# A decoder trunk whose feed-forward first parts go from six feature tiles to five, with the lambda vectors in another buffer

## The chip, the cores and the metric

The kernel runs on one core of a Trainium2 chip. The core has five engines that work side by side: TensorE (PE in the profile; its weight loads are shown apart as PEld), VectorE (DVE), ScalarE (ACT), GpSimd (POOL) and SyncE (SP), which here only issues transfers. The metric is the device time of the whole program in microseconds, as the median of its runs. One execution was also recorded by the hardware profiler; every row of the profile comes from that one.

## The reference

Two layers, each with two gated feed-forward blocks (FFNs) of half weight around a token mixer. The sequence is 512 long, the model width 1024, the FFN width 2816.

```python
def swiglu(h, w_gate, w_up, w_down):
    return (jax.nn.silu(h @ w_gate) * (h @ w_up)) @ w_down

for l in range(DEPTH):                                   # DEPTH = 2
    x = x + 0.5 * swiglu(rms_norm(x, ffn1_norm[l]), ffn1_w_gate[l], ffn1_w_up[l], ffn1_w_down[l])
    h = rms_norm(x, mix_norm[l])
    a, g, q, k, v = jnp.split(h @ w_in[l], splits, axis=-1)
    conv_out = conv_module(a, g, conv_w[l], conv_b[l], conv_norm[l])
    ...
    lam = (jnp.exp(jnp.sum(lambda_q1[l] * lambda_k1[l]))
           - jnp.exp(jnp.sum(lambda_q2[l] * lambda_k2[l])) + lam_init)
    diff_out = diff_attention(q, k, v, rel_bias, lam, lam_init, subln_norm[l])
    x = x + jnp.concatenate([conv_out, diff_out], axis=-1) @ w_out[l]
    x = x + 0.5 * swiglu(rms_norm(x, ffn2_norm[l]), ffn2_w_gate[l], ffn2_w_up[l], ffn2_w_down[l])
```

So there are four FFNs, and the lambda vectors are needed only in the mixers.

## The kernel before

**Layout and precision.** The activations stay on the chip with the features on the partitions: x is 8 tiles of 128 x 512 (`x[:, k, :]`). Every large product is done three times in a reduced format, as high x high, high x low and low x high: ScalarE makes the high part as a copy, VectorE the low part as a difference (`parts_of`, L95 to L97), for the weights as they arrive and for the activations (`acth`, `actl`; `hh`, `hl`). Weights come through rings of five raw buffers (`wraw`) and four split ones (`whi`, `wlo`), and a pair of smaller ones (`wraw2`, `whi2`, `wlo2`).

**An FFN** (`ffn`, L399) handles its 22 feature tiles of 128 in three parts, listed in `PARTS`. For each part it first makes the gated hidden tiles (gate and up products, silu, product), keeps them as `hh0, hl0, hh1, ...`, and then multiplies them with the down weights: for each of the 8 output tiles m it sums the part's feature tiles in one PSUM bank (`ps_d`) and adds the result to x (L465). `gather` (L105) collects the down weights eight blocks at a time, in the order of their use, so a block of weights can end within an output tile.

**Plain and seven-product tiles.** The feature tiles of the first part (`m < PLAIN`) are plain: gate and up are two products over 8 tiles of the input with 512 columns each (`products`). They use x times the gain without the row scale; the scale `r` is multiplied in when they leave PSUM (L443, L445). The tiles of the later parts use `seven` (L352): the input is cut into halves in features and in positions, and a 2 x 2 block product of gate and up is done with seven products of 4 tiles and 256 columns. For it `sums` (L120) loads and adds weights, with one accumulating DMA and two adds on GpSimd (L137, L142, L143), and `Halves` (L311) makes the sums of the input: eight scaled tiles `hn` (L328), and from them `th` and `tl` (L332 to L337). `settle` (L339) later overwrites `acth` and `actl` with the split of `hn`, once the plain tiles have read the old ones. This VectorE and ScalarE work runs beside the plain tiles and the first down.

**The scale of the rows.** `rows_rstd` (L206) turns the sums of squares round on TensorE (`ps_rows`), adds them on VectorE (`rowv`, L214 and L215) and takes the power on GpSimd (`rs_y`, L203). `spread` (L218) puts the result on a diagonal (`diag`, L230; a high and a low one when split) and multiplies by ones (`ps_spread`, L234), so that ScalarE can copy the scale of each position to all partitions (`rb`, L238). In the first FFN it stands in the middle of the third tile's second product, before its fourth step; its place in TensorE's order is pinned.

**Once, in the first FFN.** When it reaches feature tile 4, `ffn` calls `make_scalars` (L492) and `make_bias` (L472). `make_scalars` loads, for each layer, the four lambda vectors by a GpSimd DMA (`lamv`, L498), multiplies them on GpSimd (L500), sums them on VectorE (L502) and takes the exponential on ScalarE (L504). The buffer of `lamv` is that of `ssum`, the sums of squares, and there is one of it.

**Order.** The program is written in plain order. A planner with its own estimate of durations then sets the order of the instructions on each engine, apart from a few matmuls that are pinned, and adds the waits. Each engine and each DMA queue takes its instructions in that order. PSUM has two banks each for three tags (`sc`, `po`, `mm`) that tiles and down products use in turn.

Of the kernel before, what the change touches and what calls it, by code (L numbers as in the profile page):

```python
# [11 lines left out]
F32 = mybir.dt.float32  # L12
# [6 lines left out]
P = 128  # L19
DEPTH = 2  # L20
SEQ = 512
# [19 lines left out]
HS = SEQ // 2  # L41


PARTS = ((0, 6), (6, 8), (14, 8))
PLAIN = PARTS[0][1]

SPACE = 392
# [14 lines left out]
def lambda_init(layer):  # L62
    return 0.8 - 0.6 * math.exp(-0.3 * layer)
# [3 lines left out]
def trunk(ctx: ExitStack, tc: tile.TileContext, xt, par, lamv, relb, onehot,  # L67
# [7 lines left out]
    wp = ctx.enter_context(tc.tile_pool(name="wp", bufs=1))  # L75
    tmp = ctx.enter_context(tc.tile_pool(name="tmp", bufs=2))
# [3 lines left out]
    def f32(ap):  # L80
        return ap.bitcast(F32)
# [96 lines left out]
    for half in range(2):  # L178
        h, kk = slice(half * 512, (half + 1) * 512), range(half * KT // 2, (half + 1) * KT // 2)
# [16 lines left out]
    def col(l, name, i=0):  # L196
        c = _AT[name] + i
        return pars[l][:, c : c + 1]
# [42 lines left out]
    class Prep:  # L241


        def __init__(self, l, gain):
            self.l, self.gain = l, gain
            self.hi, self.lo = acth, actl
            self.s = tmp.tile([P, SEQ], F32, tag="ssum", name="ssum", bufs=1)
# [63 lines left out]
    class Halves:  # L311
# [4 lines left out]
        def __init__(self, fp, pr, r):  # L316
            self.th = fp.tile([P, 3, KT // 2, HS], F32R, tag="th", name="th")
            self.tl = fp.tile([P, 3, KT // 2, HS], F32R, tag="tl", name="tl")

            self.whole = []  # L320
            free = [(fp, tag, 1) for tag in ("hh6", "hh7", "hl6", "hl7")]
            free += [(wp, tag, 2) for tag in ("whi2", "wlo2") for _ in range(2)]
            a, b = slice(0, HS), slice(HS, SEQ)
            for j in range(KT // 2):
                for k in (j, j + KT // 2):
                    pool, tag, bufs = free.pop()
                    h = pool.tile([P, SEQ], F32, tag=tag, name="hn", bufs=bufs)
                    V.scalar_tensor_tensor(h, x[:, k, :], col(pr.l, pr.gain, k), r, op0=ALU.mult, op1=ALU.mult)  # L328
                    self.whole.append((k, h))
                (_, ha), (_, hb) = self.whole[-2:]  # L330
                t = fp.tile([P, 3, HS], F32, tag="ht", name="ht", bufs=2)
                V.tensor_tensor(t[:, 1], hb[:, b], ha[:, b], op=ALU.subtract)  # L332
                V.tensor_tensor(ha[:, b], ha[:, a], ha[:, b], op=ALU.subtract)
                V.scalar_tensor_tensor(t[:, 0], ha[:, b], -1.0, hb[:, b], op0=ALU.mult, op1=ALU.subtract)
                V.scalar_tensor_tensor(t[:, 2], t[:, 0], -1.0, hb[:, a], op0=ALU.mult, op1=ALU.subtract)
                S.activation(self.th[:, :, j, :], t, AF.Copy)
                V.tensor_tensor(self.tl[:, :, j, :], t, f32(self.th[:, :, j, :]), op=ALU.subtract)  # L337
# [61 lines left out]
    def ffn(pr, gu, dn, after, lead=None, aside=None):  # L399
        with tc.tile_pool(name="ffn", bufs=1) as fp:  # L400
            r = halves = None
            for m0, many in PARTS:
                hh, held, late = [], [], []
# [88 lines left out]
    def make_scalars():  # L492
        for l in range(DEPTH):

            t = tmp.tile([P, SEQ], F32, tag="ssum", name="lamv", bufs=1)
            lv = t[:, : 4 * HD].rearrange("p (n d) -> p n d", n=4)
            pr = t[:, 4 * HD : 6 * HD].rearrange("p (n d) -> p n d", n=2)
            nc.gpsimd.dma_start(lv, lamv[l].partition_broadcast(P))  # L498
            for n in range(2):
                G.tensor_tensor(pr[:, n, :], lv[:, 2 * n, :], lv[:, 2 * n + 1, :], op=ALU.mult)  # L500
            d = small.tile([P, 2], F32, tag="lamd", name="lamd", bufs=1)
            V.tensor_reduce(d, pr, axis=AX.X, op=ALU.add)  # L502
            e = small.tile([P, 2], F32, tag="lame", name="lame", bufs=1)
            S.activation(e, d, AF.Exp)  # L504
            nl = const.tile([P, 1], F32, tag=f"nlam{l}", name=f"nlam{l}")
            V.scalar_tensor_tensor(nl, e[:, 1:2], -lambda_init(l), e[:, 0:1], op0=ALU.add, op1=ALU.subtract)
            nlam.append(nl)
            g = const.tile([P, 2], F32, tag=f"gq{l}", name=f"gq{l}")
            G.memset(g, 0.0)
            for m in range(2):  # L510
                d = slice(m * HD, (m + 1) * HD)
                G.tensor_tensor(g[d, m : m + 1], col(l, "q_norm")[d], col(l, "k_norm")[d], op=ALU.mult)
            G.tensor_scalar(g, g, -math.sqrt(HD), None, op0=ALU.mult)
            gq.append(g)
            g = const.tile([P, 1], F32, tag=f"gsub{l}", name=f"gsub{l}")
            G.tensor_scalar(g, col(l, "subln_norm"), math.sqrt(VD) * (1.0 - lambda_init(l)), None, op0=ALU.mult)
            gsub.append(g)
            g = const.tile([P, CT], F32, tag=f"ghalf{l}", name=f"ghalf{l}")
            c = _AT["conv_norm"]
            G.tensor_scalar(g, pars[l][:, c : c + CT], 0.5, None, op0=ALU.mult)  # L520
            ghalf.append(g)
            c = _AT["conv_w"]
            G.tensor_scalar(pars[l][:, c : c + CT * TAPS], pars[l][:, c : c + CT * TAPS], 0.5, None, op0=ALU.mult)
# [298 lines left out]
    def aside():  # L822
        make_scalars()
        make_bias()
# [92 lines left out]
```

## Time and profile before

| what | value |
|---|---|
| median of three runs | 1805.56 us (1805.36 to 1805.93) |
| the profiled execution | 1803.93 us, of which the span is 1802.1 us |
| TensorE | busy 99% of the span, 10,692 matmuls, granted clock 1.00 |
| VectorE, ScalarE, GpSimd | 67%, 49%, 36% |
| DMA | 228 MB, 127 GB/s on average |

The busy time of an engine is a sum over the span; a matmul's listed duration is its latency, and matmuls follow each other faster than that. In the chain of work that ended last, a piece stands with its start, its length and its instructions. In the list of waits, a row names the engine, the tile and line that waited, then what released it, and total time, count and longest wait. In the rows in order of time, the bracket at the end gives the engine's idle time before the row and what ended it.

### The profile page before, as it was taken

The numbers are of one execution on the slowest core, as the hardware profiler recorded it, in microseconds if no ns is written. First come the engines' busy times: TensorE is split into PE (matmuls) and PEld (weight loads), VectorE is DVE, ScalarE is ACT, GpSimd is POOL, SyncE is SP. The second block draws the span as 40 slices with busy tenths as digits, with TensorE's granted clock in tenths as the row PEclk, the third lists the DMA queues.
The fourth block names the chain that finished last, engine by engine and source line by source line (L and its number), as shares of the span: only waits on it lengthen the run. The fifth ranks groups of instructions, "written<-read, shape, count | busy, mean of one in ns | idle before, by whom it ended". The sixth has DMA issues, their size and how long they took to land.

```text
span 1802.1 us, 27871 instructions
## 1 busy us (share of the span) xinstructions
PE 1785.1 (99%) x10692; PEld 1584.0 (88%) x10692; DVE 1200.5 (67%) x1838; ACT 883.3 (49%) x1450; POOL 640.3 (36%) x448
## 2 busy tenths in 40 slices
PE   8999999999999999999999999999999999999999
PEld 6899899888778889899888998998887888998997
DVE  6957466568867857557576684665788587575662
ACT  5546345445854436346434462554558354463551
POOL 4125123269942024133100341332797330241320
PEclk9999999999999999999999999999999999999999
DMA  6456456333212446546333574654231133564561
GB/s 229 127 129 184 134 152 175 117 105 94 71 46 84 111 112 175 164 124 188 121 94 106 128 200 107 171 169 129 71 108 56 48 105 96 146 179 132 152 174 49
DMA packets 106022, 228.06 MB, mean 127 GB/s; under 512 B 11575, under 2 KB 29254, under 8 KB 105888
## 3 DMA queue, kind: packets, MB, share of 16 engines
q1 hardware_dynamic: 86880, 190.88, 32.7%
q0 software_dynamic: 18720, 35.23, 12.0%
q8 instruction: 84, 1.38, 0.3%
q14 instruction: 50, 0.41, 0.1%
q10 hardware_dynamic: 288, 0.16, 0.0%
HBM read 224.12 MB, written 3.42 MB: 126 GB/s over the span
## 4 chain that ended last, share of the span: by engine, by line
PE 95%; DVE 2%; issue 1%; ACT 1%; DMA 0%; POOL 0%; ACTq 0%; DVEq 0%; POOLq 0%
PE ps_pair L369 36%; PE ps_d L163 9%; PE ps_d L159 9%; PE ps_d L162 9%; PE ps_pair L163 6%; PE ps_pair L162 6%; PE ps_pair L159 6%; PE ps_pair L582 2%; PE ps_pair L583 2%; PE ps_pair L581 2%; PE ps_out L159 1%; PE ps_out L162 1%; PE ps_sc L699 1%; PE ps_out L163 1%; DVE actl L252 1%; PE ps_v L611 1%
## 5 line engine op out<-in xcount | busy, mean ns | idle before, releaser
L96 ACT ACTIVATE whi<-wraw 128x512 fp32r<-128x512 f32 (+1 forms) x580 | 458.7, 814 | 643.7 <-PE ps_d L162 225.7
L97 DVE TENSOR_TENSOR wlo<-wraw,whi 128x512 fp32r<-128x512 f32 (+1 forms) x536 | 510.4, 974 | 191.3 <-ACT whi L96 186.2
L369 PE MATMUL ps_pair<-acth,wlo 128*128 128x256 f32 x1024 | 289.8, 283 | 0.0
L369 PE MATMUL ps_pair<-actl,whi 128*128 128x256 f32 x1024 | 289.8, 283 | 0.0
L369 PE MATMUL ps_pair<-acth,whi 128*128 128x256 f32 x1024 | 289.7, 283 | 0.0
L162 PE MATMUL ps_d<-hl,whi 128*128 128x512 f32 x704 | 274.0, 389 | 0.0
L163 PE MATMUL ps_d<-hh,wlo 128*128 128x512 f32 x704 | 272.7, 389 | 0.0
L159 PE MATMUL ps_d<-hh,whi 128*128 128x512 f32 x704 | 268.7, 389 | 0.0
L137 POOL DMA_DIRECT2D wraw<-in_gu x64 | 76.3, 1193 | 457.8 <-DMA wraw<-in_gu 209.9
L369 PE MATMUL ps_pair<-th,wlo 128*128 128x256 f32 x768 | 217.3, 283 | 0.0
L369 PE MATMUL ps_pair<-tl,whi 128*128 128x256 f32 x768 | 217.2, 283 | 0.0
L369 PE MATMUL ps_pair<-th,whi 128*128 128x256 f32 x768 | 217.2, 283 | 0.0
L142 POOL TENSOR_TENSOR wraw<-wraw 128x512 f32<-128x512 f32 x64 | 95.5, 1492 | 314.9 <-DMA wraw<-in_gu 277.2
L159 PE MATMUL ps_pair<-acth,whi 128*128 128x512 f32 x512 | 200.0, 394 | 5.8 <-ACT whi L96 5.7
L162 PE MATMUL ps_pair<-actl,whi 128*128 128x512 f32 x512 | 200.4, 392 | 0.3 <-DVE actl L252 0.2
L163 PE MATMUL ps_pair<-acth,wlo 128*128 128x512 f32 x512 | 199.6, 391 | 0.7 <-DVE wlo L97 0.7
L369 PEld LDWEIGHTS ps_pair<-actl,whi 128*128 128x128 f32 x1024 | 196.6, 192 | 0.3
L369 PEld LDWEIGHTS ps_pair<-acth,whi 128*128 128x128 f32 x1024 | 196.6, 192 | 0.3
L369 PEld LDWEIGHTS ps_pair<-acth,wlo 128*128 128x128 f32 x1024 | 196.6, 192 | 0.0
L465 DVE SCALAR_TENSOR_TENSOR x<-ps_d,x 128x512 f32<-128x512 f32 x96 | 65.0, 688 | 196.0 <-PE ps_d L163 196.0
L163 PEld LDWEIGHTS ps_d<-hh,wlo 128*128 128x128 f32 x704 | 132.2, 188 | 27.0
L159 PEld LDWEIGHTS ps_d<-hh,whi 128*128 128x128 f32 x704 | 132.2, 188 | 26.9
(172 smaller groups left out, 3316.6 us busy)
## 6 DMA issues: line engine op xcount, KB each, us to landing
wraw<-in_gu SPq DMA_DIRECT2D x108, 512.0 KB, 3.6
wraw<-in_gu SPq DMA_DIRECT2D x200, 256.0 KB, 4.1
wraw<-in_gu POOLq DMA_DIRECT2D x64, 512.0 KB, 5.8
wraw<-in_wqkv SPq DMA_DIRECT2D x24, 512.0 KB, 3.6
wraw<-in_dn SPq DMA_DIRECT2D x52, 192.0 KB, 3.3
wraw<-in_wag SPq DMA_DIRECT2D x16, 512.0 KB, 3.7
wraw<-in_wout SPq DMA_DIRECT2D x16, 512.0 KB, 3.6
wraw<-in_dn SPq DMA_DIRECT2D x24, 320.0 KB, 3.5
```

The costliest lines, as they stand in the source:

```text
L96: S.activation(hi, raw, AF.Copy)
L97: (eng or V).tensor_tensor(out=lo, in0=raw, in1=f32(hi), op=ALU.subtract)
L137: nc.gpsimd.dma_start(two.rearrange("p (b c) -> p b c", b=2), u[:, h[0]].unsqueeze(1).broadcast_to([P, 2, 512]), accum_op=ALU.add)
L142: G.tensor_tensor(more[:, h[0]], two[:, h[1]], whole[:, h[0]], op=ALU.add)
L159: first = T.matmul(ps, wh, xh, start=start, stop=False)
L162: T.matmul(ps, wh, xl, start=False, stop=False)
L163: T.matmul(ps, wl, xh, start=False, stop=stop)
L369: mm = T.matmul(ps, l, r, start=first and i == j == 0, stop=False, skip_group_check=True)
L465: V.scalar_tensor_tensor(x[:, m, :], ps, 0.5, x[:, m, :], op0=ALU.mult, op1=ALU.add)
L581: T.matmul(ps[n], xh[:, t], wh, start=k == 0, stop=False)
L582: T.matmul(ps[n], xh[:, t], wl, start=False, stop=False)
L583: T.matmul(ps[n], xl[:, t], wh, start=False, stop=k == KT - 1)
```

## The change

`PARTS` becomes 5, 8 and 9 feature tiles. So feature tile 5 is no longer plain but a seven-product tile, in the second part, and the third part starts a tile earlier and has nine. With nine tiles there are buffers `hh8` and `hl8`. The eight `hn` tiles of `Halves` take `hh5` to `hh8` and `hl5` to `hl8`, which the first part does not use; before, four of them had lain in the two buffers each of `whi2` and `wlo2`. The lambda vectors take the buffer of the (high) diagonal, of which there is also one.

```diff
-PARTS = ((0, 6), (6, 8), (14, 8))
+PARTS = ((0, 5), (5, 8), (13, 9))
 PLAIN = PARTS[0][1]
...
             self.whole = []
-            free = [(fp, tag, 1) for tag in ("hh6", "hh7", "hl6", "hl7")]
-            free += [(wp, tag, 2) for tag in ("whi2", "wlo2") for _ in range(2)]
+            free = [f"{t}{n}" for t in ("hh", "hl") for n in range(5, 9)]
             a, b = slice(0, HS), slice(HS, SEQ)
             for j in range(KT // 2):
                 for k in (j, j + KT // 2):
-                    pool, tag, bufs = free.pop()
-                    h = pool.tile([P, SEQ], F32, tag=tag, name="hn", bufs=bufs)
+                    h = fp.tile([P, SEQ], F32, tag=free.pop(), name="hn")
                     V.scalar_tensor_tensor(h, x[:, k, :], col(pr.l, pr.gain, k), r, op0=ALU.mult, op1=ALU.mult)
...
     def make_scalars():
         for l in range(DEPTH):
 
-            t = tmp.tile([P, SEQ], F32, tag="ssum", name="lamv", bufs=1)
+            t = tmp.tile([P, SEQ], F32, tag="diag", name="lamv", bufs=1)
             lv = t[:, : 4 * HD].rearrange("p (n d) -> p n d", n=4)
```

## The prediction

> **What bounds the kernel now.** I read the page's busy shares first, then the chain that ended last, then TensorE's waits, and then the stretches that the change touches.
>
> ```profile
> PE 1785.1 (99%) x10692; PEld 1584.0 (88%) x10692; DVE 1200.5 (67%) x1838; ACT 883.3 (49%) x1450; POOL 640.3 (36%) x448
> PE 95%; DVE 2%; issue 1%; ACT 1%; DMA 0%; POOL 0%; ACTq 0%; DVEq 0%; POOLq 0%
> PE ps_pair L159 <- ACT whi L96: 5.7, 1, 5.7
> PE ps_out L159 <- ACT acth L683: 2.5, 2, 1.3
> PE ps_spread L234 <- DVE diag L230: 1.8, 1, 1.8
> ```
>
> TensorE is busy 99% of the span and carries 95% of the chain. Its longest waits are the start (5.7 us) and, for this change, 1.8 us for the first scale's diagonal. So the end moves with the number of matmuls times their spacing, and with any new wait on TensorE. The stretches around the parts, and one of plain matmuls:
>
> ```profile
> 50.00:91.00 41.00, 41.00 (x182) 33.50 (x181) 36.25 (x62) 22.71 (x33) 5.69 (x6) 1.00 0.47 136
> 112.00:200.00 88.00, 88.00 (x706) 86.70 (x705) 59.10 (x87) 50.28 (x86) 28.81 (x18) 1.00 0.63 170
> 236.00:325.00 89.00, 89.00 (x710) 87.52 (x709) 59.12 (x85) 49.59 (x85) 28.14 (x18) 1.00 0.61 164
> 50.03 0.39 PE L163 MATMUL ps_pair<-acth,wlo 128*128 128x512 f32 x1
> 56.83 0.39 PE L163 MATMUL ps_pair<-acth,wlo 128*128 128x512 f32 x1
> 112.16 76.31 PE ps_pair L369 x636
> 1673.95 76.31 PE ps_pair L369 x636
> ```
>
> The columns of the first three are the stretch, its length, then busy time with the instruction count for TensorE, its weight loads, VectorE, ScalarE and GpSimd, then granted clock, DMA share and GB/s. TensorE is full in the end of the plain part (50 to 91) and in both parts of eight seven-product tiles (from 112 and 236), at clock 1.00, with DMA at 0.61 to 0.63. VectorE is the nearest other engine only in the plain part: 36.25 of 41 us.
>
> **The swap of one tile in each of four FFNs.** Feature tile 5 changes from plain to seven products. Plain is 2 x 8 x 3 = 48 matmuls of 512 columns. From 50.03 to 56.83 lie 30 of them: 6.80 / 30 = 0.2267 us each, 10.88 us per tile (their 0.39 us is latency, which overlaps). Seven products are 7 x 4 x 3 = 84 matmuls of 256 columns: 76.31 / 636 = 0.120 us, 10.08 us per tile. The gain is 0.80 us, and 4 x 0.80 = 3.2 us. The down products stay 22 x 8 x 3 per FFN (5 + 8 + 9 against 6 + 8 + 8), so their PE time does not move.
>
> The Trainium skill, "TensorE: Matmul & The Clock Gate", section "Back-to-back issue gap", speaks against the swap by one of its rules: a sustained stream is spaced by weight load and matmul together, with 81 ns for 128 columns and 131 ns for 512; an estimate on a straight line between them gives 98 ns for 256, 8.2 us for 84 against 6.3 us for 48, a loss of 1.9 us per tile. The section's other rule, the isolated gap of 518 and 262 cycles, makes 10.4 against 9.2 us, at 2.4 GHz, an estimate of 4.8 us gained in all. The trace agrees with the sign of the second and is 5 to 10% above its gaps.
>
> **What the extra seven-product tiles bring beside TensorE.** Per FFN: one more accumulating DMA and two adds on GpSimd, six splits on ScalarE and on VectorE in place of two, and 0.75 MB more of weights than the plain tile's 1 MB. They run at the end of a part whose eight tiles show TensorE full at the DMA share and VectorE share above, so nothing lands on the path: zero. If that cover failed, the price would be the wait of one tile's operands; none shows in the eight such parts (the chain has eight runs of 636 matmuls in 76.31 us, the first and the last above), and I keep 1 us per FFN as an upper end. The down weights need 20 more SP issues, since runs of five and nine blocks are cut differently; each is short and hidden by the five-deep ring:
>
> ```profile
> wraw<-in_dn SPq DMA_DIRECT2D x36, 64.0 KB, 2.7
> ...
> 42.42 0.69 DVE L443 TENSOR_TENSOR gs<-ps_pair,rb 128x512 f32<-128x512 f32 x1
> 87.22 0.69 DVE L409 TENSOR_TENSOR hl<-gs,hh 128x512 fp32r<-128x512 f32 x1
> ...
> 79.35 0.39 PE L159 MATMUL ps_d<-hh,whi 128*128 128x512 f32 x1
> ...
> 616.39 0.68 DVE L409 TENSOR_TENSOR hl<-gs,hh 128x512 fp32r<-128x512 f32 x1
> ...
> 624.53 0.39 PE L159 MATMUL ps_d<-hh,whi 128*128 128x512 f32 x1
> ```
>
> A 64 KB load takes 2.7 us, against 5.4 us (24 x 0.2267) for the products of one gathered block of weights.
>
> **The shorter first part: the tight place.** VectorE makes the halves' operands in the plain part whatever its length, while TensorE loses 10.9 us of plain products to hide them. Before, the first FFN's VectorE work from the first eviction (42.42) to the last hl (87.91) is 73 instructions in 45.5 us, 0.62 us each. TensorE began the down products at 79.35 and did those of the first five tiles until hl came. In the changed order the same stretch has 61 instructions (one tile's evictions, a few chunk splits and part of the settling fall out or move back): 38 us. It begins 2.2 us sooner (below), at 40.2, so the fifth tile's hl is there at 78.2. TensorE begins the down at 79.35 - 10.9 - 2.2 = 66.3, and its order puts 66 matmuls of the four other tiles over five banks ahead of the first that needs this hl: 66.3 + 66 x 0.2267 = 81.2. Slack 3 us, cost zero. In the other three FFNs the scale is known before the third tile, and the slack is larger. In the second, the fifth tile's hl ended at 617.07 with its products done at 624.53 - 10.88 = 613.65, where the down now begins; 49 matmuls stand ahead of its use, at 624.8. Slack 7.7 us.
>
> ```profile
> 101.75 1.29 DVE L97 TENSOR_TENSOR wlo<-wraw,whi 128x512 fp32r<-128x512 f32 x2 [1.11 <-ACT whi L96]
> 111.99 0.28 PE L369 MATMUL ps_pair<-acth,whi 128*128 128x256 f32 x1
> 112.19 0.69 DVE L465 SCALAR_TENSOR_TENSOR x<-ps_d,x 128x512 f32<-128x512 f32 x1 [3.06 <-PE ps_d L163]
> ```
>
> **From the first down to the first seven-product tile.** Before, the first pair of sums is split at 101.75 to 103.04 and needed at 111.99, 9 us ahead. The down shrinks from 144 to 120 matmuls, 5.4 us less cover. The splits follow the weights' ring, whose places free with the same down products, so the lead stays; if it did not, 3.5 us are left: zero. The bank of the last down tile is evicted at 112.19 to 112.88, and the second product, 12 x 0.12 us after 111.99, writes there at 113.43: 0.55 us. The changed order has the same 12 matmuls there and nothing new ahead of that eviction on VectorE. Zero, with 4 x 0.6 us as the upper end.
>
> **The halves' buffers.** The eight hn tiles move from four places of hh/hl and four of whi2/wlo2 to eight of hh/hl (5 to 8), free until the second part. So the u2 splits of the first two seven-product tiles no longer wait for the settling. In the first FFN they move, in ScalarE's and VectorE's order, ahead of the third tile's chunks, into idle time of 10.00 and 5.83 us; in the others to the end of the FFN before:
>
> ```profile
> 28.74 3.91 ACT L96 ACTIVATE whi<-wraw 128x1024 fp32r<-128x1024 f32 x4 [10.00 <-PE ps_pair L162]
> 29.83 2.36 DVE L97 TENSOR_TENSOR wlo<-wraw,whi 128x1024 fp32r<-128x1024 f32 x2 [5.83 <-ACT whi L96]
> ```
>
> Two splits of 0.6 to 0.7 us fit: zero.
>
> **The lambda vectors.** This is the one wait that goes. Columns: start, duration, piece of the chain; then the engines' own rows:
>
> ```profile
> 32.00 5.91 DMA lamv<-in_lamv
> 37.99 0.59 POOL lamv L500 x2
> 38.58 1.02 POOL rs_y L203
> 39.99 0.61 DVE diag L230
> ...
> 34.98 0.16 DVE L215 TENSOR_SCALAR rowv<-rowv 128x4 f32<-128x4 f32 x1
> 39.91 0.68 DVE L230 TENSOR_TENSOR diag<-ident,rc_hi 128x512 fp32r<-128x512 f32 x1
> ...
> 38.55 0.39 PE L163 MATMUL ps_pair<-acth,wlo 128*128 128x512 f32 x1
> 40.74 1.01 PE L234 MATMUL ps_spread<-diag,ones_r 128*128 128x512 f32 x2 [1.80 <-DVE diag L230]
> 41.59 0.40 PE L159 MATMUL ps_pair<-acth,whi 128*128 128x512 f32 x1
> ...
> 571.14 0.16 DVE L215 TENSOR_SCALAR rowv<-rowv 128x4 f32<-128x4 f32 x1
> 573.34 0.17 DVE L223 TENSOR_SCALAR rc_hi<-rs_y 128x4 fp32r<-128x4 f32 x1 [0.91 <-POOL rs_y L203]
> 574.22 0.69 DVE L230 TENSOR_TENSOR diag<-ident,rc_lo 128x512 fp32r<-128x512 f32 x1
> 577.81 0.40 PE L234 MATMUL ps_spread<-diag,ones_r 128*128 128x512 f32 x1
> 578.05 0.39 PE L159 MATMUL ps_pair<-acth,whi 128*128 128x512 f32 x1
> ```
>
> The row sums were ready at 35.14, but on GpSimd's in-order queue rs_y stood behind the lambda products, which waited for their DMA until 37.99. In the buffer of the diagonal the vectors cannot be loaded before the spread has read it, so rs_y now comes first. Without that queue the second FFN shows the path: 571.30 to rc_hi 2.04 us, to the second diagonal's end (574.91) 3.6 us. From 35.14 that is 38.75, and the first diagonal 0.6 us before. TensorE arrives at 38.55 + 0.227 = 38.78 for the first spread and 39.0 for the second; before, the first spread followed its diagonal's end (40.59) by 0.15 us. So the wait goes. From 38.55 to 41.59 are 3.04 us; one matmul (0.227) and two spreads (577.81 to 578.05, 0.24 each) need 0.71. Gain 2.33; as the second diagonal has 0.1 us to spare I take 2.2. Ends: 0, should another hand-over take the wait's place, and 2.33.
>
> Behind it on GpSimd: the first one-hot DMA now precedes the lambda DMA, so the bias matmul (16 matmuls on) has its operand sooner. The first lambda DMA waits for the spread (39.4), lands some 5.9 us on; the second waits for VectorE to reduce the first, near 49, and VectorE meets its result near 55 with up to 1 us of wait. ScalarE loads the exp table in the middle of the evictions, as it did before for the second vector. All of this eats into the 3 us above, and who waits for it is that hl; no more.
>
> **Sum.** 3.2 + 2.2 = 5.4 us. The profiled execution has a span of 1802.1 and 1803.93 us in all, so 1798.5; it lies 1.63 us below the median of the three runs, 1805.56, and against that the forecast is 1800.2 us (1805.56 - 5.4), 0.30% faster. A change under 0.2%, 3.6 us, I count as none.
>
> **The rivals.**
> 1. The scale's path is no shorter, because rs_y, a hand-over or the spread's place takes the wait's turn. For it: only 0.1 us is left at the second diagonal. Against: the row sums stood ready for 2.8 us with GpSimd waiting. Then only the swap counts: 1802.4.
> 2. Slower: the fifth tile's hl comes late in all four FFNs and TensorE waits in the first down, because VectorE's work for the halves has lost a tile of cover. It decides once VectorE is later than the slack of 3 us (7.7 in the others); to be over 0.2% slower each FFN must lose (5.4 + 3.6) / 4 = 2.25 us beyond that: 1809.2. For it: VectorE's 36.25 of 41 us. Against: the larger slack of three FFNs.
> 3. The first seven-product tile's operands or bank come late at each of the shrunken downs: 0.6 to 1 us per FFN, 1802.6 to 1804.2. For it: 0.55 us at the bank. Against: the same order there.
> 4. The plain tile is the cheaper one, since weight loads set the spacing of short matmuls:
>
> ```profile
> L369 PEld LDWEIGHTS ps_pair<-actl,whi 128*128 128x128 f32 x1024 | 196.6, 192 | 0.3
> ```
>
> At 0.192 us each, 84 would take 16.1 us, 5.2 lost per tile, 1805.56 + 21.0 - 2.2 = 1824.4. Against: the run of 636 holds both, load and matmul, at 0.120 us. It is the first rule of the Trainium skill's page above, with this row's duration.
>
> **Chances.** Forecast 0.74; rival 1 0.10; rival 2 0.08; rival 3 0.06; rival 4 0.01; 0.01 for another loss. Faster: 0.74. Within: rivals 1 and 3, 0.16. Slower: 0.10. The range is 1799.0 to 1803.2: below by 1.2 us for what a new order may remove of TensorE's other waits, above past rival 1 and the lower half of rival 3. It leaves out rivals 2 and 4.
>
> **What would show it.** Right: 10,836 matmuls instead of 10,692; TensorE's wait for the diagonal gone from the list of waits and rs_y directly behind rowv; runs of seven-product matmuls of 84 more in one part, still at 0.120 us; no TensorE wait at ps_d in the first part. Wrong: a wait of ps_d for hl, of ps_pair L367 for whi or for a bank, or a first scale that still holds TensorE near 38 us.

## The result, and the profile after

The changed kernel takes 1799.15 us (median of seven runs, 1798.44 to 1801.19), against 1804.39 of the kernel before (seven runs, 1803.63 to 1805.93; the three shown earlier are its highest). The ratio is 0.9970, with an interval of 0.9959 to 0.9982: 0.3% faster. By the medians the gain is 5.24 us, against 5.4 forecast; the time itself lies 1.05 us below the forecast of 1800.2. The profiled execution took 1801.19 us with a span of 1799.4 and is the slowest of the seven.

The page of the changed kernel, its engines and the chain that ended last:

```profile
PE 1782.5 (99%) x10836; PEld 1588.6 (88%) x10836; DVE 1225.8 (68%) x1858; ACT 895.1 (50%) x1478; POOL 644.3 (36%) x460
PE 92%; DVE 2%; DMA 2%; issue 1%; ACT 1%; POOL 0%; POOLq 0%; SPq 0%; ACTq 0%; DVEq 0%
```

TensorE has 144 matmuls more and 2.6 us less of busy time. New on the chain is DMA with 2%. TensorE's waits:

```profile
PE ps_pair L159 <- ACT whi L96: 5.6, 1, 5.6
PE ps_out L159 <- ACT acth L681: 2.5, 2, 1.3
PE ps_pair L367 <- DVE wlo L97: 1.6, 2, 0.8
...
PE ps_pair L367 <- ACT whi L96: 0.3, 1, 0.3
```

The wait for the diagonal is gone. The lines with L367 are new: seven-product tiles whose weights come late, 1.9 us in all. There is no wait at `ps_d`. The first scale in order of time: GpSimd, the second diagonal on VectorE, then TensorE:

```profile
35.06 1.04 POOL L203 TENSOR_TENSOR rs_y<-rowv,mhalf 128x4 f32<-128x4 f32 x1 [13.77 <-DVE rowv L215]
36.08 0.67 POOL L477 DMA_DIRECT2D oneh<-in_onehot  x1
39.35 0.58 POOL L496 DMA_DIRECT2D lamv<-in_lamv  x1 [2.60 <-PE ps_spread L234]
...
37.03 0.68 DVE L230 TENSOR_TENSOR diag<-ident,rc_lo 128x512 fp32r<-128x512 f32 x1
...
38.41 0.40 PE L163 MATMUL ps_pair<-acth,wlo 128*128 128x512 f32 x1
38.64 0.64 PE L234 MATMUL ps_spread<-diag,ones_r 128*128 128x512 f32 x2
39.12 0.40 PE L159 MATMUL ps_pair<-acth,whi 128*128 128x512 f32 x1
```

`rs_y` stands right behind `rowv`, the lambda transfer behind the spread, and the products go on at 39.12 instead of 41.59. Next the chain's runs of seven-product matmuls, in order of time, and the stretches of the first FFN (columns as in the prediction):

```profile
93.40 76.31 PE ps_pair L367 x636
289.42 17.29 PE ps_pair L367 x142
640.78 76.31 PE ps_pair L367 x636
764.97 86.39 PE ps_pair L367 x720
...
1655.77 86.39 PE ps_pair L367 x720
```

```profile
110.00:200.00 90.00, 90.00 (x650) 85.46 (x649) 59.74 (x83) 45.73 (x76) 22.57 (x16) 1.00 0.61 165
218.00:305.00 87.00, 85.07 (x705) 84.46 (x704) 66.28 (x89) 50.98 (x90) 28.66 (x21) 1.00 0.62 163
```

The parts of nine run 720 matmuls (84 more than 636) in 86.39 us, still 0.120 each, except in the first FFN, where the run is broken: 1.93 us of TensorE are missing between 218 and 305. The chain inside that part (start, duration, piece; short pieces between these are left out), and then from GpSimd's own rows the issue at 257.83:

```profile
230.17 0.33 SPq L132
230.54 5.79 DMA wraw<-in_gu
236.89 8.39 DMA wraw<-in_gu
245.52 1.28 POOL wraw L142
246.88 1.56 POOL wraw L143
248.44 5.49 DMA wraw<-in_gu
254.16 1.31 POOL wraw L142
255.49 0.64 ACT whi L96
256.16 1.56 DVE wlo L97
257.83 7.63 DMA wraw<-in_gu
265.70 1.29 POOL wraw L142
...
277.99 9.32 DMA wraw<-in_gu
...
257.83 1.20 POOL L137 DMA_DIRECT2D wraw<-in_gu  x1 [0.68 <-DVE wlo L97]
```

It is a loop: add, add, accumulating transfer of the next tile (5.49), add, split, and only when that split has ended the accumulating transfer of the tile after (257.83). From 245.52 to 265.70 it takes 20.18 us for two tiles; TensorE needs 20.16 for two. So the feed runs as fast as its user, with nothing to catch up a late start, and a slow transfer goes straight into the next wait: the following round, from 265.70 to 287.55, takes 21.85 us, since its second transfer takes 9.32 and not 7.63. TensorE's 1.9 us are 0.78 at 247.40, near the start of the first of these two rounds, and 0.30 and 0.84 after the second. The last link, VectorE and GpSimd beside each other, and TensorE:

```profile
288.05 3.00 DVE L97 TENSOR_TENSOR wlo<-wraw,whi 128x512 fp32r<-128x512 f32 x2 [3.20 <-ACT whi L96]
```

```profile
287.55 1.26 POOL L142 TENSOR_TENSOR wraw<-wraw 128x512 f32<-128x512 f32 x1 [8.35 <-DMA wraw<-in_gu]
288.89 1.61 POOL L143 TENSOR_TENSOR wraw<-wraw 128x512 f32<-128x512 f32 x1
```

```profile
288.07 0.39 PE L367 MATMUL ps_pair<-acth,whi 128*128 128x256 f32 x1 [0.30 <-ACT whi L96]
289.42 0.39 PE L367 MATMUL ps_pair<-acth,wlo 128*128 128x256 f32 x1 [0.84 <-DVE wlo L97]
```

Two splits take 3.00 us while GpSimd adds; TensorE waits 0.84 us for a split and, just before, 0.30 us for the copy ahead of it.

### The profile page after: what moved, and what is told of

It reads as the page before. It is cut to its first block, busy times and chain, and to the rows that moved or that the text cites. A ratio compares the mean times of both kernels' runs of the same rounds, so it can differ in the third digit from the quotient of the medians.

```text
span 1799.4 us, 28320 instructions
## 1 busy us (share of the span) xinstructions
PE 1782.5 (99%) x10836; PEld 1588.6 (88%) x10836; DVE 1225.8 (68%) x1858; ACT 895.1 (50%) x1478; POOL 644.3 (36%) x460
## 4 chain that ended last, share of the span: by engine, by line
PE 92%; DVE 2%; DMA 2%; issue 1%; ACT 1%; POOL 0%; POOLq 0%; SPq 0%; ACTq 0%; DVEq 0%
PE ps_pair L367 35%; PE ps_d L163 9%; PE ps_d L162 9%; PE ps_d L159 9%; PE ps_pair L163 5%; PE ps_pair L162 5%; PE ps_pair L159 5%; DMA wraw<-in_gu 2%; PE ps_pair L581 2%; PE ps_pair L580 2%; PE ps_pair L579 2%; PE ps_sc L697 2%; PE ps_out L162 1%; PE ps_out L163 1%; PE ps_out L159 1%
## 5 line engine op out<-in xcount | busy, mean ns | idle before, releaser
L97 DVE TENSOR_TENSOR wlo<-wraw,whi 128x512 fp32r<-128x512 f32 (+1 forms) x552 | 540.6, 1001 | 206.3 <-ACT whi L96 201.5
L367 PE MATMUL ps_pair<-acth,wlo 128*128 128x256 f32 x1088 | 308.1, 283 | 1.6 <-DVE wlo L97 1.6
L367 PE MATMUL ps_pair<-acth,whi 128*128 128x256 f32 x1088 | 307.9, 283 | 0.3 <-ACT whi L96 0.3
L367 PE MATMUL ps_pair<-actl,whi 128*128 128x256 f32 x1088 | 307.9, 283 | 0.0
L367 PE MATMUL ps_pair<-th,wlo 128*128 128x256 f32 x816 | 230.9, 283 | 0.0
L367 PE MATMUL ps_pair<-tl,whi 128*128 128x256 f32 x816 | 230.8, 283 | 0.0
L367 PE MATMUL ps_pair<-th,whi 128*128 128x256 f32 x816 | 230.8, 283 | 0.0
L367 PEld LDWEIGHTS ps_pair<-acth,wlo 128*128 128x128 f32 x1088 | 208.8, 192 | 2.0 <-DVE wlo L97 2.0
L367 PEld LDWEIGHTS ps_pair<-acth,whi 128*128 128x128 f32 x1088 | 208.8, 192 | 0.8 <-ACT whi L96 0.5
L367 PEld LDWEIGHTS ps_pair<-actl,whi 128*128 128x128 f32 x1088 | 208.8, 192 | 0.3
L159 PE MATMUL ps_pair<-acth,whi 128*128 128x512 f32 x448 | 175.3, 395 | 5.6 <-ACT whi L96 5.6
L162 PE MATMUL ps_pair<-actl,whi 128*128 128x512 f32 x448 | 175.7, 393 | 0.3 <-DVE actl L252 0.2
L163 PE MATMUL ps_pair<-acth,wlo 128*128 128x512 f32 x448 | 174.9, 391 | 0.5 <-DVE wlo L97 0.5
L367 PEld LDWEIGHTS ps_pair<-tl,whi 128*128 128x128 f32 x816 | 156.5, 192 | 0.7
L367 PEld LDWEIGHTS ps_pair<-th,whi 128*128 128x128 f32 x816 | 156.5, 192 | 0.6
```

The source lines that it names most:

```text
L97: (eng or V).tensor_tensor(out=lo, in0=raw, in1=f32(hi), op=ALU.subtract)
L159: first = T.matmul(ps, wh, xh, start=start, stop=False)
L162: T.matmul(ps, wh, xl, start=False, stop=False)
L163: T.matmul(ps, wl, xh, start=False, stop=stop)
L367: mm = T.matmul(ps, l, r, start=first and i == j == 0, stop=False, skip_group_check=True)
```

## The experiments

Times are medians; each run's kernel before was run on the same chip and took 1804.0 to 1804.6 us.

### The change again, and its two halves

`again` is the changed kernel. `diag_alone` is the kernel before with the second edit only, `parts_alone` the changed kernel without it:

```diff
-            t = tmp.tile([P, SEQ], F32, tag="ssum", name="lamv", bufs=1)
+            t = tmp.tile([P, SEQ], F32, tag="diag", name="lamv", bufs=1)
```

> The changed kernel itself once more. Theory A, the stall of TensorE in the nine-tile part of the first FFN (1.9 us in the profile after, 245 to 290 us) is a matter of slow transfers in that one execution: the new profile shows TensorE full from 200 to 330 us (over 129.7 of 130) and the span comes out near 1797. Theory B, it belongs to the program (the loop that loads and adds the weights of a seven-product tile needs more than TensorE's 10.08 us per tile there): again 1 to 2 us of waits of ps_pair L367 for whi or wlo near 245 to 290 us, and a span near 1799. Time by either against the kernel before: 4.5 to 6 us less, as in the runs seen.

> The kernel before, parts of 6, 8 and 8, with only the lambda vectors moved to the diagonal's buffer. Theory A (the prediction's): the wait for the first diagonal goes and nothing takes its place, 2.2 to 2.5 us less than before. Rival: the gain is given back later in the first FFN, because the two lambda transfers now land after the spread and VectorE and ScalarE wait for them before the evictions and the splits that the down needs: under 1 us less, with a new wait of TensorE between 50 and 100 us.

> The changed kernel with the lambda vectors back in the buffer of the sums of squares: only the parts of 5, 8 and 9 and the places of hn are new. Theory A: 4 x 0.80 = 3.2 us less than before, and with the first FFN's stall of up to 1.9 us where it shows, 1.3 to 3.2 less. Rival: the fifth tile's low part comes late in the first down when the scale comes 2.4 us later (the prediction's slack of 3 us in the first FFN): a wait at ps_d near 80 us, and under 1.3 us less.

| kernel | time (lowest to highest) | ratio to before (interval) |
|---|---|---|
| again | 1799.11 (1798.50 to 1800.57) | 0.9967 (0.9956 to 0.9979) |
| diag_alone | 1801.84 (1801.55 to 1802.02) | 0.9983 (0.9974 to 0.9992) |
| parts_alone | 1799.91 (1799.68 to 1801.03) | 0.9973 (0.9962 to 0.9984) |

In the profile of `again` the stall is there and smaller (list of waits):

```profile
PE ps_pair L367 <- DVE wlo L97: 0.4, 1, 0.4
```

Its time was 1799.60; less 0.4 it is 1799.2, and 1801.19 less 1.9 is 1799.3. So the stall is not one execution's alone, and its size changes with the execution: it lies between what theories A and B expected (none, or 1 to 2 us). From 205 to 292 us the 256 KB loads took 5.5 us there (median), 6.0 in the first profile, and 4.4 in that of `parts_alone`, which has no such wait at all.

`diag_alone` brings 2.8 us against that call's median and 2.4 between the two profiled executions (1803.93 to 1801.55): theory A, with nothing given back. `parts_alone` brings 4.7, more than the 3.2 of the swap and than the 1.3 to 3.2 expected. Its list of waits tells most of why:

```profile
PE ps_spread L234 <- DVE diag L230: 0.6, 1, 0.6
```

Here the lambda transfer landed in 4.7 us instead of 5.9, so 1.2 us of the diagonal's wait were gone already. So the halves overlap, and 2.8 + 4.7 is more than the 5.5 of both. Why the transfer was quicker in this execution is open; five profiles of the kernel before (below) have it at 5.4 to 6.0.

### What makes the stall in the part of nine

`old_places` returns the `hn` tiles to `hh6, hh7, hl6, hl7` and the `whi2`, `wlo2` buffers. `nine_second` has the parts the other way round:

```diff
-PARTS = ((0, 5), (5, 8), (13, 9))
+PARTS = ((0, 5), (5, 9), (14, 8))
```

`own_more` gives the two added weight tiles a buffer in the FFN's pool, so that a tile takes two places of the ring and not three (`sums` gets `fp` as an argument). `adds_vector` instead puts the two adds on VectorE:

```diff
-        more = ring("wraw")
+        more = fp.tile([P, 1024], F32, tag="more", name="more")
```

```diff
-        G.tensor_tensor(more[:, h[0]], two[:, h[1]], whole[:, h[0]], op=ALU.add)
-        G.tensor_tensor(more[:, h[1]], more[:, h[0]], whole[:, h[1]], op=ALU.add)
+        V.tensor_tensor(more[:, h[0]], two[:, h[1]], whole[:, h[0]], op=ALU.add)
+        V.tensor_tensor(more[:, h[1]], more[:, h[0]], whole[:, h[1]], op=ALU.add)
```

> The changed kernel with the eight hn tiles in the places of before (hh6, hh7, hl6, hl7 and the four of whi2 and wlo2). Theory A: the places matter little, the time is that of the changed kernel within 0.5 us. Rival: the early split of the next FFN's first u2 tiles, which the new places allow, loads the end of the nine-tile part and causes its stall: then no wait of ps_pair L367 between 245 and 290 us here, and up to 2 us less than the changed kernel. Second rival: u2 splits that wait for the settling hold up the first seven-product tile: a wait of ps_pair L367 near 93 us or at the same place in the other FFNs, and 0.5 to 4 us more than the changed kernel.

> The changed kernel with the two added weight tiles (`more`) in a buffer of the FFN's own, so that a seven-product tile takes two places of the five-deep wraw ring and not three. Theory C: the stall in the nine-tile part of the first FFN is the loop load, accumulating transfer, two adds, accumulating transfer, add, split, load, which goes round once per two tiles because a ring of five has no room for two tiles of three; in the profile after it takes 20.18 us (245.52 to 265.70) against 20.16 of TensorE. With two places per tile it is cut open: no wait of ps_pair L367 between 200 and 330 us, a span at or below 1797.4, and runs that agree within 1 us; median 1797.5 to 1798.7. Rival D (the transfers of that stretch are slow by themselves, whatever the ring): waits of 0.4 to 1.9 us stay.

> The changed kernel with the two adds of the weights on VectorE in place of GpSimd; the ring is as in the changed kernel. Theory E: the stall comes from VectorE's splits, which take 0.93 us on average there in place of 0.69 and up to 1.8 when a GpSimd add runs beside them. Then no split of 128 x 512 is longer than 0.75 us, the loop shrinks by 2 to 3 us per two tiles, no wait of ps_pair L367 stays in the first FFN, median 1797.5 to 1798.7. Rival: VectorE, at 8.3 us of 10 in that stretch and now with 1.4 us more work less the 1.2 us or so of the drawn-out splits, takes its work in an order in which the add waits for a transfer and the splits stand behind it: new waits of TensorE and a time above 1800.

> The changed kernel with parts of 5, 9 and 8: the part of nine is the second. If nine tiles in a part make the stall, it moves to 105 to 200 us and is gone from 220 to 310; if the third part of the first FFN is where the loop of the ring runs without a lead, whatever its length, waits of 0.4 to 2 us of ps_pair L367 stay at 235 to 300 in some executions; if it is one execution's slow transfers, there may be none. Time within 1 us of the changed kernel by all of them.

> The changed kernel with hn in its old places and the added tiles in their own buffer. If the two remove the same thing, the nine-tile part's stall, this is as own_more, 1798.5 to 1799.3, with runs within 1 us of each other. If the old places gained something else (0.4 us between the medians of old_places and own_more), it keeps that: 1798.2 to 1798.7.

| kernel | time (lowest to highest) | TensorE's wait at L367, first FFN |
|---|---|---|
| the change (two profiles) | 1799.1 (1798.44 to 1801.19) | 1.9 and 0.4 |
| old_places | 1798.72 (1798.23 to 1799.38) | none |
| own_more | 1799.18 (1799.02 to 1799.28) | none |
| nine_second | 1798.34 (1798.20 to 1799.05) | none |
| old_places_own_more | 1798.39 (1798.16 to 1798.83) | none |
| adds_vector | 1968.24 (1966.49 to 1971.62) | (see below) |

(One execution of `own_more` took 5334.37 us and is left out of its row.) The looser ring of `own_more` leaves no wait, and its runs lie within 0.3 us of each other, as theory C expects; its median is 0.5 us above the 1797.5 to 1798.7 that theory C gave. The stall's price on the median is small: the four kernels without it lie 0.1 us above to 0.8 us below the change. `nine_second` shows that nine tiles in a part do not make it: both parts of its first FFN are full (stretches as above),

```profile
110.00:200.00 90.00, 90.00 (x694) 87.38 (x692) 61.21 (x90) 50.16 (x86) 30.48 (x19) 1.00 0.64 176
...
220.00:310.00 90.00, 90.00 (x697) 87.59 (x696) 58.60 (x85) 48.10 (x84) 29.96 (x21) 1.00 0.62 164
```

and `old_places`, with the nine last, has none either, in one profile. So theory C holds as far as a loop without slack goes. That the transfers' time decides which executions fall behind fits the three profiles above, but no run varies it alone, and why they are slow in some is open. That `old_places` gains by its places is not shown: 0.4 us is less than the spread of the change.

`adds_vector` did the opposite of theory E's forecast. Groups by line, first in the changed kernel between 224 and 300 us, then in `adds_vector` over the span:

```profile
L97 DVE TENSOR_TENSOR wlo<-wraw,whi 128x512 fp32r<-128x512 f32 x37 | 34.3, 947 | 16.5 <-ACT whi L96 15.7
```

```profile
L97 DVE TENSOR_TENSOR wlo<-wraw,whi 128x512 fp32r<-128x512 f32 x348 | 232.6, 698 | 48.6 <-ACT whi L96 48.5
```

Without adds on GpSimd no split is drawn out (698 ns against 947). But in `own_more` the splits of `wraw` are as slow (909 ns) and nothing stalls, so the drawn-out split is a link of the stall and not its cause. And the rival came true by far, 169 us slower (ratio 1.0909, 1.0895 to 1.0924). VectorE's waits there:

```profile
DVE wraw L142 <- DMA wraw<-in_gu: 265.9, 56, 8.6
```

GpSimd had spent that waiting time for nothing else; on VectorE every split and eviction stands behind it.

### One plain tile less again

`plain_four` has parts of 4, 9 and 9, `plain_four_own_more` that and the separate buffer.

> The changed kernel with parts of 4, 9 and 9: one more tile of each FFN goes from plain to seven products. Theory A: 4 x 0.80 = 3.2 us less than the changed kernel, 1795.9, if VectorE's work for the halves still fits: after the change the fifth tile's hl is ready at 75.08 and TensorE needs it near 81, 6 us of slack; without a further tile TensorE comes 10.9 us sooner and VectorE about 7.5, so 2.6 us are left. Rival C: both nine-tile parts of the FFNs now meet the loop of the wraw ring at 10.1 us per tile: waits of ps_pair L367, 0.5 to 2 us in each of several parts, 1796 to 1801. Rival: the fifth part of the cover was the last and ps_d waits for hl or L367 for the settling, 2 to 5 us per FFN: 1803 and more.

> Parts of 4, 9 and 9 with the added tiles in their own buffer. If the loop of the ring (theory C) is what limits the parts of nine, this is 3.2 us below own_more, 1794.3 to 1795.5, with no wait of ps_pair L367 inside a part. If the cover of the halves' work is what limits it, it loses as much against own_more as plain_four does against the changed kernel.

They take 1809.50 us (ratio 1.0030, 1.0018 to 1.0041) and 1809.53 us (1.0026, 1.0016 to 1.0036): 10.4 us above the change, not 3.2 below. The looser ring doesn't help in all, so it is the cover. Waits and then stretches of `plain_four`:

```profile
PE ps_pair L367 <- DVE x L463: 7.8, 4, 3.1
...
PE ps_d L159 <- ACT hh L406: 1.8, 1, 1.8
PE ps_d L159 <- DVE gs L441: 1.4, 1, 1.4
```

```profile
60.00:70.00 10.00, 8.21 (x35) 6.44 (x36) 10.00 (x20) 3.79 (x6) 2.95 (x3) 1.00 0.31 82
84.00:87.00 3.00, 2.63 (x12) 2.66 (x13) 2.13 (x3) 0.00 (x0) 2.92 (x2) 0.51 0.94 298
```

In the first FFN VectorE is full (10.00 of 10) and TensorE waits for the evictions at the down's start, for a hidden tile, and for the last down bank: 1.4 + 1.8 + 3.1 = 6.3 us. The three others lose 4.7 together at the bank. With 3.2 gained that makes 7.8; more comes from the clock, which was 0.51 after the longest wait, so that 12 matmuls took 2.63 us instead of 1.44. The rest of the 10.4 isn't accounted for. In `plain_four_own_more` the same loss lies elsewhere: TensorE waits 5.3 and 3.1 us in the first FFN, and in the three others only 0.9 us together at the bank; there too the clock fell, to 0.50 and 0.51 behind the two long waits.

### A version that beats both

`mixed` is `own_more` with four plain tiles in the last three FFNs only, and there the first part's down products one bank tag further:

```diff
-PLAIN = PARTS[0][1]
+FOUR = ((0, 4), (4, 9), (13, 9))
...
+            parts = PARTS if lead else FOUR
-            for m0, many in PARTS:
+            for m0, many in parts:
...
-                    if m >= PLAIN:
+                    if m >= parts[0][1]:
...
-                    ps = bank(turn_tag(m0 + many + m // 2), "ps_d")
+                    ps = bank(turn_tag(m0 + many + m // 2 + (many == 4)), "ps_d")
```

> Own_more with parts of 4, 9 and 9 in the last three FFNs, 5, 8 and 9 in the first, and there the down products of the four-tile part one bank tag further, so that the last two no longer use the banks of the first seven-product tile. In plain_four these three FFNs lost 1.57 us each waiting for that bank and gained 0.80; the first lost 6.3. If the bank is the only thing that is short, TensorE loses nothing there and the time is 3 x 0.80 = 2.4 us below own_more: 1796.8. If the rest of VectorE's queue (splits, settling) is what is late, a wait of ps_pair L367 for another releaser or of ps_d stays, 1 to 2 us per FFN: 1799.8 to 1803.

1796.10 us (1795.95 to 1797.04), ratio 0.9954 (0.9941 to 0.9966): the fastest kernel here, 3.1 us below `own_more`, where 2.4 were expected; the other 0.7 are open. No wait at L367 or `ps_d` is left. As the separate buffer by itself left 0.9 us at the banks, the other bank tag can hardly have brought more than that. The stretches around the first down of the first FFN and of the second:

```profile
50.00:105.00 55.00, 55.00 (x289) 47.07 (x288) 43.40 (x73) 28.21 (x44) 16.91 (x14) 1.00 0.56 147
590.00:650.00 60.00, 60.00 (x377) 54.50 (x376) 53.01 (x75) 32.06 (x53) 18.53 (x13) 1.00 0.60 144
```

In the second FFN VectorE has 53.01 of 60 us, and it still suffices. That this is because the scale is known earlier there is argued and not tested.

### Where the kernel before scatters, and another way round its wait

`before_again` and `before_p1` to `before_p3` are the kernel before. `lamv_early` gives the lambda vectors a buffer of their own, so that the first transfer is issued at 1.34 us:

```diff
-            t = tmp.tile([P, SEQ], F32, tag="ssum", name="lamv", bufs=1)
-            lv = t[:, : 4 * HD].rearrange("p (n d) -> p n d", n=4)
-            pr = t[:, 4 * HD : 6 * HD].rearrange("p (n d) -> p n d", n=2)
+            t = tmp.tile([P, 4 * HD], F32, tag="lamv", name="lamv", bufs=1)
+            lv = t.rearrange("p (n d) -> p n d", n=4)
+            pr = lv[:, 0::2, :]
```

`diag_own_more` is `diag_alone` with the buffer of `own_more`.

> The kernel before, for a second profile. Theory F: its scatter (1803.3 to 1806.2, against 1801.5 to 1802.0 with the lambda vectors in the diagonal's buffer) is the wait for the lambda transfer, which takes its own time in each execution: 5.9 us from issue to landing and 1.8 us of wait for the diagonal in the profile at 1803.93, 4.7 and 0.6 in that of parts_alone. Then here, too, the time less the wait for the diagonal is 1802.1 within 0.5 us. Rival: the scatter is from elsewhere, and the wait is 1.8 us whatever the time.

> Theory F: the time less the wait for the diagonal (list of waits, ps_spread) is 1802.1 to 1802.2 again, so at 1805 or more the wait is 2.9 us or more. Rival: the wait is 1 to 2 us whatever the time, and what is over lies in the first 30 us (transfers of the first tiles) or elsewhere.

> As before_p1: time less the wait for the diagonal 1802.1 to 1802.2 by theory F; by the rival the wait stays at 1 to 2 us.

> As before_p1: time less the wait for the diagonal 1802.1 to 1802.2 by theory F; by the rival the wait stays at 1 to 2 us.

> The kernel before with a buffer of its own for the lambda vectors (the two products overwrite the first and third vector), so that their transfer is issued in the first microseconds and nothing waits for it at the scale. Theory F (before's scatter is the wait for this transfer): 1801.3 to 1802.3, as with the diagonal's buffer, all runs within 1 us, and no wait for the diagonal. Rival (the diagonal's buffer gains by what it moves behind the spread, or the scatter is from elsewhere): a scatter of 2 to 3 us as before, or a time apart from diag_alone's by over 0.7 us.

> Parts of 6, 8 and 8 with the lambda vectors in the diagonal's buffer and the added weight tiles in their own: diag_alone with a looser ring. Against own_more (1799.18) it differs in the parts and the places of hn alone. Theory A: 3.2 us more than own_more, 1802.4, or, as the starts of the runs differ by up to 0.6 us, 1801.5 to 1802.6. If the ring's loop also held back parts of eight, it is faster than diag_alone by over 0.5 us: under 1801.3.

| execution of before | time | wait for the diagonal | time less wait |
|---|---|---|---|
| the first profile | 1803.93 | 1.8 | 1802.1 |
| before_again | 1803.40 | 1.2 | 1802.2 |
| before_p1 | 1804.26 | 1.9 | 1802.4 |
| before_p2 | 1804.08 | 1.7 | 1802.4 |
| before_p3 | 1803.86 | 1.7 | 1802.2 |

The wait follows the time to within 0.3 us over these five. None of them lies above 1805, so theory F is not shown for the high executions. That the two kernels with the diagonal's buffer and the old parts scatter by 0.5 and 0.9 us, and before by 3.5, speaks for it; that `lamv_early`, which has no such wait, scatters by 1.8 speaks against.

`lamv_early` took 1804.29 us (1803.44 to 1805.28; ratio 1.0000, 0.9991 to 1.0009), nothing gained, and theory F's number for it was wrong. The spans of its runs are 0.6 us shorter than those of before (medians 1801.7 and 1802.3), but 2.1 to 3.3 us of each execution lie outside the span, against 1.7 to 1.8 before; what they are is open. The wait for the diagonal is gone, and another is there:

```profile
PE ps_pair L159 <- ACT whi L96: 7.6, 2, 5.9
...
PE ps_pair L162 <- DVE actl L252: 0.7, 1, 0.7
```

```profile
x<-in_xt SPq DMA_DIRECT2D x8, 256.0 KB, 6.9
wraw<-in_gu SPq DMA_DIRECT2D x8, 256.0 KB, 6.0
...
lamv<-in_lamv POOLq DMA_DIRECT2D x1, 128.0 KB, 6.8
```

The second fence lists the transfers of the first 12 us: beside the lambda vectors the first loads land in 6.9 and 6.0 us; before it was 5.2 for both. TensorE lost 1.65 us more between its first products. So the diagonal's buffer gains by the place it gives the transfer, behind the scale, and not by taking it from ahead of the scale alone.

`diag_own_more` took 1801.41 us (1801.10 to 1802.03): 0.4 below `diag_alone`, just between the two ranges expected, so the ring hardly holds back parts of eight. From here to `old_places_own_more`, which differs from it in `PARTS` alone, are 3.0 us; to `own_more`, which has other places for `hn` too, 2.2. TensorE's busy time falls by 3.4 in `own_more` (1784.9 to 1781.5). The swap's 3.2 is about right; of what is missing in `own_more`, 0.45 us lie in its first 50 us, where TensorE has that much less of work done than in `diag_own_more`.

## Why the prediction was right, and where it was wrong

**The swap (3.2 us): right.** 10,836 matmuls, 0.120 us at both lengths of part, and 3.0 us of time between two kernels that differ in `PARTS` alone (2.2 where the places of `hn` differ too). Rival 4, whose price came from the weight loads, has nothing for it.

**The lambda vectors (2.2 us): right.** The rows give 2.47 (41.59 to 39.12, of which 0.14 is TensorE's earlier arrival), the profiled times of `diag_alone` 2.4. Rival 1 is out for this edit. Its ground, 0.1 us to spare at the second diagonal, was a mis-sized path: from the row sums (34.98) to that diagonal's end (37.71) the rows show 2.73 us and not the 3.6 read from the second FFN, where `rs_y` took 1.92 us instead of 1.04; TensorE arrived at 38.64, 0.9 us after the diagonal's end. And the reason for the gain was told too simply: `lamv_early` has the transfer out of the scale's way as well and gains nothing. Where the transfer runs counts too, and at the start it runs beside the first loads.

**"What the extra seven-product tiles bring beside TensorE ... nothing lands on the path: zero": wrong.** The step argued from parts in which TensorE was full and from DMA and VectorE shares of 0.6 and two thirds. Shares don't show a loop: the ring's round takes 20.18 us for two tiles against TensorE's 20.16, and with slow transfers TensorE lost 1.9 us in the profiled execution and 0.4 in the next. The upper end, "1 us per FFN", was too low for the first FFN. Where the stall didn't come, the zero held.

**"It lies 1.63 us below the median of the three runs, 1805.56, and against that the forecast is 1800.2": wrong.** This is the step that put the number 1.05 us too high, and not the gain, which was 5.24 us where 5.4 were forecast. The three runs were the highest of the seven: over all seven the median is 1804.39, 1.17 us lower, and 5.4 off that is 1799.0. The later runs agree with the lower base: 1804.62 over the 18 runs of the next comparison, and 1804.0 to 1804.2 in the later ones. Laid on the profiled execution, the forecast is the 1798.5 that the same paragraph gives. Why the three were high is not shown; a longer wait for the diagonal, which the change removes, is theory F, and no execution above 1805 was profiled. The kernels without the stall took 1798.3 to 1799.2, and 6 of the 13 runs of the change lie below 1799.0, where the range began.

**The shorter first part: right, and closer to the edge than its slack says.** No wait at `ps_d`; the fifth tile's low part was done at 75.08 us:

```profile
74.41 0.67 DVE L407 TENSOR_TENSOR hl<-gs,hh 128x512 fp32r<-128x512 f32 x1
```

That is 3 us before the 78.2 of the working. Yet one tile less costs 6.3 us of waits in the same place: rival 2's mechanism decides one step further on, and only in the first FFN, as `plain_four` and `mixed` show. Rival 3's bank (0.55 us of slack, no wait here) is what lost 4.7 us in `plain_four`.

## What to carry to other kernels

A share of busy time does not tell whether a feed keeps up: go round the ring once (load, accumulate, add, split, place free again) and compare that time with the user's, tile for tile. A forecast of a time is no better than its base: three runs stood 1.17 us above the seven, a fifth of the whole gain, while the gain itself was right to 0.2 us. Cover is used up in a step, not a slope: five plain tiles hid everything, four cost 6.3 us of waits in the FFN whose scale comes late and, with the looser ring and the other banks of `mixed`, none in the others, so that the split is worth choosing stage by stage.

## What the runs showed of the hardware

**A VectorE split takes longer beside a GpSimd add.** Two splits of 128 x 512 took 3.00 us beside two adds (1.26 and 1.61 us); in `adds_vector`, without adds of weights on GpSimd, the mean of 348 was 0.698. The Trainium skill, "SBUF — State Buffer", section "SBUF: two separate sides", states that a GpSimd operation and a VectorE operation with two inputs in SBUF take a shared port pair exclusively for a whole instruction. These rows agree: 3.00 us is about two splits of 0.7 and one add of 1.6.

**TensorE's clock halves after a wait of 3.1 us.** In order of time, `plain_four`:

```profile
84.37 0.55 PE L367 MATMUL ps_pair<-acth,whi 128*128 128x256 f32 x1 [3.09 <-DVE x L463]
```

This wait was followed by a granted clock of 0.51 for the next 3 us, and matmuls of 0.22 us instead of 0.120; in `plain_four_own_more` a wait of 3.09 us was followed by 0.51 as well; waits of 1.4 and 1.8 us left it at 1.00. The Trainium skill, "TensorE: Matmul & The Clock Gate", section "What's actually happening", gives half rate after an idle window of about 3.4 us; the half agrees, and here 3.09 us were already enough.

**Loads were slower beside a 128 KB transfer from GpSimd's queue.** The lambda vectors of a layer go to all 128 partitions; in `lamv_early`, at the start, that took 6.8 us, and the 256 KB loads beside it 6.0 and 6.9 (medians) instead of 5.2, in one profile of each kernel.
